# Zero-filled 128-row products for the 16-token block, and two shifted rope chains, in a four-layer hybrid kernel on one core

## The chip, the cores and the metric

The kernel runs on one core of a Trainium2 chip. The metric is the device time of one execution in microseconds. TensorE (PE) does the matrix products, VectorE (DVE), ScalarE (ACT) and GpSimd (POOL) the elementwise work, and SyncE (SP) issues the DMAs. In the profile the loading of a product's stationary operand (its weights) is a row of its own, PEld.

## The reference

1024 tokens are preceded by 16 learned meta tokens, so the sequence that counts has 1040 tokens, width 1024. Four layers follow each other; each adds its branch to the residual stream, and the 16 meta tokens are dropped at the end.

```python
h = concat(zeros(112), meta(16), x(1024))          # blocks of 128; the first holds 16 valid tokens
for i in range(4):
    u = rmsnorm(h, norm_gain[i])
    y = (attention_branch, mlstm_branch, hgrn2_branch)[i % 3](u, ...)
    h = h + where(valid, y, 0)
return h[:, 128:]

# attention (layers 0 and 3): 16 heads of 64, 4 k/v heads, window 128 inside and across blocks
q = rope(rmsnorm(q, q_gain), pos); k = rope(rmsnorm(k, k_gain), pos)
p = softmax over this block and the one before, with a sink per head
o = p @ v ;  y = (o * silu(z)) @ w_out
# mlstm (layer 1): 8 heads, keys 128, values 256, chunks of one block, state C (128 x 256) and n (128)
num = w_inter * (q @ C) + qk @ v ;  C = w_old * C + (w_s * k)^T @ v
# hgrn2 (layer 2): 8 heads, keys 128, values 128, state S (128 x 128)
o = (q * exp(A)) @ S + att @ v ;  S = exp(A_last) * S + k'^T @ v
```

## The kernel before

Everything is kept with channels on partitions and tokens on the free axis, in three chunks of tokens (400, 384 and 256 columns). The 1040 tokens are nine blocks: block 0 with the 16 meta tokens, blocks 1 to 8 with 128 tokens each (`blk(b)` gives a block's first column and its size, `cn` or `nq`). Chunk 0 holds blocks 0 to 3.

The large products (`proj`, line 231; `proj_v`, line 280; `proj_out`, line 325) run in three parts, high times high, low times high and high times low, with operands split by ACT (`s.copy` to a rounded type, line 195) and DVE (the remainder, line 196). Weights come by DMA into `wr` (line 207).

The mixers work block by block. For block 0 they use slices of 16 partitions or 16 columns:

- attention, `S_step`, `T_step`, `V_step`: `S_step` makes the scores and the normalised probabilities `Sm` (its last operation is POOL's line 737), `T_step` transposes them on PE (line 749) and splits them into `Ph` and `Pl` (ACT line 751, DVE line 752), `V_step` multiplies them with the values (line 768). In layer 0 this is done for block 0 of four pairs of tiles and two halves; layer 3 leaves block 0 out, because its queries are dropped.
- mlstm, `mixer` of `layer_b`: `s1` makes `W` and `kw`, `s2` multiplies `W` with the values (line 1010; for later blocks also the state, line 1012) and makes `hn`, `s3` makes the state's update from `kw` and the values (line 1024), `s4` transposes `hn` (line 1038).
- hgrn2, `mixer` of `layer_c`: `tail0` makes `att`, for block 0 in a 16x16 tile (line 1282), for the others by copies on POOL (line 1290, `att<-rd`); `kT` is the transposed key (line 1314); line 1322 makes the state's update and line 1343 the output.

The values of block 0 in layers 1 and 2 are written by `put_v` (lines 240 to 246).

PE's order is written out by hand: a layer gives lists of steps with a cost each, `chain` and `spread` put follow-up steps at a delay behind their tile, and `weave` merges lists by cost. The other engines' order follows from the order in which the steps are issued. The normalisation and rope of a k tile are three follow-up steps per chunk in `qk_proj`: `stat` (the sum of squares on PE, lines 614 and 617, and its reciprocal root on ACT, lines 341 and 342), `rope` (four DVE operations, lines 624 to 628) and `turn` (`k_split`: six ACT casts at lines 507, 508 and 510 and two DVE subtractions). Their delays behind the tile, in the units of the step costs, are `D_K0` for the first k tile of layer 0, `D_K1` for the second, and `D_K` for layer 3. For the second tile `stat` also issues the DMAs that swap halves (`turned`, line 568). The rows that a step's `stat` needs are ACT's two readings of the product, lines 574 and 575.

Of the kernel before, what the change touches and what calls it, by code (L numbers as in the profile page):

```python
# [9 lines left out]
F32 = mybir.dt.float32  # L10
# [36 lines left out]
FIRST = (1.1, 0.2, 0.85), (2.1, 1.35, 1.85)  # L47
D_K0, D_K1 = (2500.0, 5000.0, 7000.0), (4500.0, 7500.0, 9500.0)
D_Q0 = 3500.0, 7500.0, 4500.0, 6500.0
# [64 lines left out]
def hybrid_kernel(ctx: ExitStack, tc: tile.TileContext, ins, out, layers=(0, 1, 2, 3)):  # L114
# [125 lines left out]
    def put_v(V, acc, b, cn):  # L240

        if b == 0:
            s.copy(V[:cn, :256], acc[32 : 32 + cn, :256])
            v.tensor_tensor(V[:cn, :256], V[:cn, :256], acc[:cn, :256], op=ALU.add)
        else:
            s.copy(V[:cn, :256], acc[:cn, :256])
# [232 lines left out]
    def layer_a(i, j, first, last, fin, scale=None):  # L479
# [217 lines left out]
        def mixers():  # L697


            def S_step(w):  # L700
# [16 lines left out]
                S = psum("pm", 2).rearrange("p (u k) -> p u k", u=2)  # L717
                w["Sm"] = Sm = mix.tile([P, 2, 257], F32, tag="Sm", name=nm("Sm"), bufs=2)
                st, den = small(2), small(2)
                sinks = []  # L720
# [19 lines left out]
            def T_step(w):  # L740
                b, kbs, Sm = w["b"], w["kbs"], w["Sm"]
                nq = blk(b)[1]
                kn = NMETA if b == 0 else P
                pt = psum("pt", 1).rearrange("p (k u q) -> p k u q", k=2, u=2)
                w["Ph"] = Ph = R["mix"].tile([P, 2, 2, P], F32R, tag="Ph", name=nm("Ph"), bufs=2)
                w["Pl"] = Pl = R["mix"].tile([P, 2, 2, P], F32R, tag="Pl", name=nm("Pl"), bufs=2)
                for ki, (kb, ko, _) in enumerate(kbs):
                    for u in range(2):
                        pe.transpose(pt[:kn, ki, u, :nq], Sm[:nq, u, ko : ko + kn], ident[:nq, :nq])  # L749
                src, h, l = (z[:kn, : len(kbs), :, :nq] for z in (pt, Ph, Pl))  # L750
                s.copy(h, src)
                v.tensor_tensor(l, src, h.bitcast(F32), op=ALU.subtract)

            def V_step(w):
                b, kbs, hh, pair = w["b"], w["kbs"], w["hh"], w["pair"]
                q0, nq = blk(b)
                kn = NMETA if b == 0 else P
                grp = [z for z in GROUPS if b in z][0]
                g0 = blk(grp[0])[0]
                if b == grp[0]:  # L760
                    for t in w["ts"]:
                        if ("o", t) not in R:
                            R["o", t] = row()
                    R["po", hh] = psum("po", 1).rearrange("p (u q) -> p u q", u=2)
                po = R["po", hh]
                for ki, (kb, _, _) in enumerate(kbs):
                    for part in ("Ph", "Pl"):
                        pe.matmul(po[:, :, q0 - g0 : q0 - g0 + nq], V[pair // 2, kb][:kn, P * hh : P * hh + P],  # L768
                                  w[part][:kn, ki, :, :nq], start=(ki == 0 and part == "Ph"),
                                  stop=(ki == len(kbs) - 1 and part == "Pl"))  # L770
                if b == grp[-1]:
                    hs, os = slice(64 * hh, 64 * hh + 64), slice(64 - 64 * hh, 128 - 64 * hh)
                    gw = q0 + nq - g0
                    for u, t in enumerate(w["ts"]):
                        o = R["o", t][hs, g0 : g0 + gw]
                        s.copy(o, po[hs, u, :gw])
                        v.tensor_tensor(o, o, po[os, u, :gw], op=ALU.add)
# [80 lines left out]
    def layer_b(i, j, fin):  # L858
# [116 lines left out]
        def mixer(h):  # L975
# [8 lines left out]
            def s1(b):  # L984
# [10 lines left out]
                s.activation(E[:cn, :cn], E[:cn, :cn], AF.Exp)  # L995
                W["W", b] = w = mix.tile([P, P], F32, tag="W", name=nm("W"), bufs=2)
                v.tensor_tensor(w[:cn, :cn], E[:cn, :cn], pq[:cn, :cn], op=ALU.mult)
                if b:
                    W["qw", b] = qw = mix.tile([P, P], F32, tag="qw", name=nm("qw"), bufs=2)
                    v.tensor_tensor(qw, q[:, cs], R["wb"][:, cs], op=ALU.mult)  # L1000
                if b < NB - 1:
                    W["kw", b] = kw = mix.tile([P, P], F32, tag="kw", name=nm("kw"), bufs=2)
                    s.activation(kw[:cn], pq[:cn, 128:256], AF.Identity, scale=E[:cn, cn - 1 : cn])

            def s2(b):
                mix = R["mix"]
                c0, cn = blk(b)
                V = R["v", h, b]
                num = psum("po", 1)
                pe.matmul(num[:cn, :257], W["W", b][:cn, :cn], V[:cn, :257], start=True, stop=(b == 0))  # L1010
                if b:
                    pe.matmul(num[:cn, :257], W["qw", b], W["C"][:, :257], start=False, stop=True)  # L1012
                den = small(1)
                s.activation(den[:cn], num[:cn, 256:257], AF.Abs)
                v.tensor_tensor(den[:cn], den[:cn], R["em"][:cn, b, h : h + 1], op=ALU.max)
                v.reciprocal(den[:cn], den[:cn])
                W["hn", b] = hn = mix.tile([P, 256], F32, tag="hn", name=nm("hn"), bufs=2)
                s.activation(hn[:cn], num[:cn, :256], AF.Identity, scale=den[:cn])

            def s3(b):  # L1020
                mix = R["mix"]
                c0, cn = blk(b)
                pc = psa()
                pe.matmul(pc[:, :257], W["kw", b][:cn], R["v", h, b][:cn, :257], start=True, stop=True)  # L1024
                Cn = mix.tile([P, 258], F32, tag="C", name=nm("C"), bufs=2)
# [7 lines left out]
            def s4(b):  # L1033
# [3 lines left out]
                for c in range(2):  # L1037
                    pe.transpose(pt[:, c * P : c * P + cn], W["hn", b][:cn, c * P : c * P + P], ident[:cn, :cn])
                for c in range(2):
# [91 lines left out]
    def layer_c(i, j, fin):  # L1131
# [80 lines left out]
        def mixer(h):  # L1212
# [56 lines left out]
            def tail0(r):  # L1269
# [10 lines left out]
                if r == 0:  # L1280
                    att = R["mix"].tile([16, 16], F32, tag="att0", name=nm("att0"), bufs=1)
                    v.tensor_reduce(att, t6[:16, 0, f0:, :w].rearrange("p l t -> p t l"),
                                    axis=mybir.AxisListType.X, op=ALU.add)
# [22 lines left out]
            def tail1(r):  # L1306
                c0, cn = geom(r)
                bn = min(cn, P)
                pt = psum("pt", 1)
                W["kT", r] = kT = R["mix"].tile([P, 256], F32, tag="kT", name=nm("kT"), bufs=1)  # L1310
                for b in range(len(REGIONS[r])):
                    pe.transpose(pt[:bn, P * b : P * b + P], W["kA", r][:, P * b : P * b + bn], ident)
# [3 lines left out]
            def states(r):  # L1316
# [3 lines left out]
                for b in blocks:  # L1320
                    cn = blk(REGIONS[r][b])[1]
                    pe.matmul(pc[:, P * b : P * b + P], W["kT", r][:cn, P * b : P * b + P],
                              R["v", h // 2, REGIONS[r][b]][:cn, vs], start=True, stop=True)
                for b in blocks:
# [7 lines left out]
            def tail2(r, b):  # L1332
# [9 lines left out]
                att = W["att", r] if r == 0 else W["att", r][:, b, :]  # L1342
                pe.matmul(W["po"][:, oc], V[:cn, vs], att, start=True, stop=(r == 0))
                if r:
# [263 lines left out]
```

## Time and profile before

| | value |
|---|---|
| runs | 2605.04, 2612.66, 2618.38 us (median 2612.66) |
| profiled execution | 2608.14 us, of which the span is 2606.4 us |
| granted TensorE clock | 0.997 |
| PE, PEld busy | 98%, 95% of the span |
| DVE, ACT, POOL busy | 75%, 65%, 9% |

The span is the time from the first to the last instruction on the core; the profiled execution has 1.7 us around it. A row of a view by groups reads: line, engine, operation, output<-input by the program's names, the form (for PE the stationary operand's rows and columns, then the moving operand's rows and columns), the count, then busy time and mean nanoseconds of one, then the idle time of the engine just before these instructions and what ended it. "<-issue" is idle time in which the engine waited for nothing that the trace shows. A row of a timeline reads: start, length, engine, line, operation, and in brackets the idle time before it with its releaser. Within layer 1 (480 to 1500 us) PE is busy nearly without a break; most of its waits for other engines lie in layers 0, 2 and 3.

### The profile page before, as it was taken

To read this page: it belongs to the slowest core of one execution; us is meant where nothing else is said; L and a number is where in the kernel's file an instruction comes from. 1 tells how busy PE (TensorE), PEld (TensorE's weight loads), DVE (VectorE), ACT (ScalarE), POOL (GpSimd) and SP (SyncE) were. 2 spreads that over 40 slices of the span, in tenths; PEclk is the share of its full clock that TensorE was granted. 3 is DMA by queue.
4 is the path that set the end of the run, shared out by engine and by line. 5 is a ranking of instruction groups with operands and counts; after the bars stand their busy time and mean duration, and the time that the engine had idled before them with its cause. 6 is when DMAs were issued, how large, how long until landed. Compare 5 with 4: busy or idle time off the path is not lost.

```text
span 2606.4 us, 54443 instructions
## 1 busy us (share of the span) xinstructions
PE 2563.6 (98%) x20446; PEld 2486.9 (95%) x20446; DVE 1960.2 (75%) x5290; ACT 1696.1 (65%) x4434; POOL 238.9 (9%) x488
## 2 busy tenths in 40 slices
PE   8999999999999999999999999999999999999999
PEld 7998989999999999999999999999999999999999
DVE  7896898775656564747465688988888978887896
ACT  8866766566464645555545757877675857867772
POOL 0321231000000000000000000101000100321320
PEclk9999999999999999999999999999999999999999
DMA  5223212021111111111111111111111113212112
GB/s 157 62 67 93 57 44 69 30 67 58 42 53 46 49 45 54 41 58 41 50 44 54 50 35 34 34 34 34 38 38 34 34 51 88 64 44 84 56 42 77
DMA packets 86058, 140.21 MB, mean 54 GB/s; under 512 B 12425, under 2 KB 39186, under 8 KB 85794
## 3 DMA queue, kind: packets, MB, share of 16 engines
q1 hardware_dynamic: 85794, 136.73, 17.0%
q8 instruction: 161, 2.64, 0.4%
q14 instruction: 103, 0.84, 0.1%
HBM read 121.83 MB, written 4.27 MB: 48 GB/s over the span
## 4 chain that ended last, share of the span: by engine, by line
PE 79%; DVE 10%; ACT 7%; DMA 2%; issue 2%; POOL 0%; SPq 0%; DVEq 0%; ACTq 0%; POOLq 0%
PE pj L231 38%; PE pj L325 16%; PE pj L280 10%; PE po L768 2%; PE pt L749 2%; PE po L1010 1%; PE pa L1024 1%; PE po L1012 1%; DVE wl L196 1%; DVE Sm L731 1%; ACT Sm L734 1%; PE pm L723 1%; PE pm L724 1%; PE pj L276 1%; PE pm L1262 1%
## 5 line engine op out<-in xcount | busy, mean ns | idle before, releaser
L231 PE MATMUL pj<-uh,wh 128*128 128x256 f32 (+2 forms) x2688 | 915.0, 340 | 6.7 <-ACT uh L400 6.2
L231 PE MATMUL pj<-ul,wh 128*128 128x256 f32 (+2 forms) x2688 | 864.6, 322 | 0.3
L231 PE MATMUL pj<-uh,wl 128*128 128x256 f32 (+2 forms) x2688 | 864.8, 322 | 0.0
L231 PEld LDWEIGHTS pj<-uh,wh 128*128 128x128 f32 x2688 | 508.1, 189 | 23.1 <-issue 9.0
L231 PEld LDWEIGHTS pj<-ul,wh 128*128 128x128 f32 x2688 | 508.8, 189 | 6.0 <-DVE ul L196 0.8
L231 PEld LDWEIGHTS pj<-uh,wl 128*128 128x128 f32 x2688 | 507.9, 189 | 0.0
L196 DVE TENSOR_TENSOR wl<-wr,wh 128x512 fp32r<-128x512 f32 (+1 forms) x338 | 233.9, 701 | 52.4 <-ACT wh L195 48.9
L195 ACT CAST wh<-wr 128x512 fp32r<-128x512 f32 (+1 forms) x338 | 203.2, 613 | 101.4 <-PE pj L325 31.6
L325 PE MATMUL pj<-yh,wh 128*128 128x384 f32 (+2 forms) x768 | 253.7, 330 | 9.9 <-DVE x L328 7.8
L328 DVE TENSOR_TENSOR x<-x,pj 128x384 f32<-128x384 f32 (+2 forms) x480 | 234.8, 509 | 33.4 <-PE pj L325 32.1
L325 PE MATMUL pj<-yl,wh 128*128 128x384 f32 (+2 forms) x768 | 246.3, 321 | 0.1
L325 PE MATMUL pj<-yh,wl 128*128 128x384 f32 (+2 forms) x768 | 246.1, 320 | 0.0
L280 PE MATMUL pj<-wh,uh 128*128 128x256 f32 (+1 forms) x768 | 232.7, 303 | 0.0
L280 PE MATMUL pj<-wl,uh 128*128 128x256 f32 (+1 forms) x768 | 216.3, 282 | 0.0
L280 PE MATMUL pj<-wh,ul 128*128 128x256 f32 (+1 forms) x768 | 216.0, 281 | 0.0
L734 ACT ACTIVATE Sm<-Sm,s 128x257 f32<-128x257 f32 (+2 forms) x272 | 131.2, 484 | 84.6 <-DVE s L731 81.3
L737 POOL TENSOR_TENSOR Sm<-Sm,s 128x512 f32<-128x512 f32 (+2 forms) x136 | 139.4, 1025 | 419.0 <-DVE s L736 396.2
L457 ACT ACTIVATE t<-t 128x384 f32<-128x384 f32 (+2 forms) x240 | 117.8, 491 | 82.5 <-DVE t L456 80.4
L325 PEld LDWEIGHTS pj<-yh,wh 128*128 128x128 f32 x768 | 144.8, 189 | 14.1 <-DVE x L328 9.4
L195 ACT CAST yh<-r 128x384 fp32r<-128x384 f32 (+2 forms) x120 | 57.0, 478 | 149.9 <-PE pj L325 135.6
L280 PEld LDWEIGHTS pj<-wh,uh 128*128 128x128 f32 x768 | 144.7, 188 | 2.2
L280 PEld LDWEIGHTS pj<-wl,uh 128*128 128x128 f32 x768 | 144.9, 189 | 1.9
(287 smaller groups left out, 5404.5 us busy)
## 6 DMA issues: line engine op xcount, KB each, us to landing
wr<-in_b_win SPq DMA_DIRECT2D x124, 256.0 KB
wr<-in_a_win SPq DMA_DIRECT2D x80, 256.0 KB
wr<-in_c_win SPq DMA_DIRECT2D x64, 256.0 KB
wr<-in_a_wout SPq DMA_DIRECT2D x32, 256.0 KB
wr<-in_b_wout SPq DMA_DIRECT2D x32, 256.0 KB
t<-t SPq DMA_DIRECT2D x100, 48.0 KB
cs<-in_rope SPq DMA_DIRECT2D x11, 400.0 KB
cs<-in_rope SPq DMA_DIRECT2D x11, 384.0 KB
```

The lines of the kernel that those rows point to most:

```text
L195: s.copy(h, src)
L196: v.tensor_tensor(l, src, h.bitcast(F32), op=ALU.subtract)
L231: pe.matmul(acc[:, :cn], a[:, k, :], b[:, k, c0 : c0 + cn], start=(k == 0 and i == 0), stop=(k == KT - 1 and i == 2))
L276: pe.matmul(acc[:48, :nc], um[0][:, k, :], m[:, kk, :], start=(k == 0 and m is wh), stop=(k == KT - 1 and m is wl))
L280: pe.matmul(acc[:cn, :nc], a[:, k, c0 : c0 + cn], m[:, kk, :], start=(k == 0 and j == 0), stop=(k == KT - 1 and j == 2))
L325: pe.matmul(acc[:, :cn], a[:, k, mc], b, start=(k == 0 and i == 0), stop=(k == 1 and i == 2))
L328: v.tensor_tensor(x[:, m, c0 : c0 + cn], x[:, m, c0 : c0 + cn], acc[:, :cn], op=ALU.add)
L457: s.activation(a[:, :cn], a[:, :cn], AF.Exp)
L734: s.activation(Sm[:nq, u, : nk + 1], Sm[:nq, u, : nk + 1], AF.Exp, scale=-1.0, bias=st[:nq, u : u + 1], accum_out=den[:nq, u : u + 1])
L737: g.tensor_tensor(Sm[:nq, :, :nk], Sm[:nq, :, :nk], den[:nq].rearrange("p (u c) -> p u c", c=1).to_broadcast([nq, 2, nk]), op=ALU.mult)
L749: pe.transpose(pt[:kn, ki, u, :nq], Sm[:nq, u, ko : ko + kn], ident[:nq, :nq])
L768: pe.matmul(po[:, :, q0 - g0 : q0 - g0 + nq], V[pair // 2, kb][:kn, P * hh : P * hh + P], w[part][:kn, ki, :, :nq], start=(ki == 0 and par ...
```

## The change

The tiles that block 0's small products read are now filled with zeros by POOL (`g.memset`), and the products take all 128 partitions, and all 128 stationary columns where they took 16. The moving operand's number of columns stays, except at line 1038, a transposition, where it becomes 128. The evictions still read the 16 rows or columns that count. The delays `D_K0` and `D_K1` are changed. Lines move by 1 to 14 in the changed file.

```diff
-D_K0, D_K1 = (2500.0, 5000.0, 7000.0), (4500.0, 7500.0, 9500.0)
+D_K0, D_K1 = (4300.0, 6300.0, 8300.0), (4400.0, 5700.0, 8500.0)
...
         if b == 0:
+            g.memset(V, 0.0)
             s.copy(V[:cn, :256], acc[32 : 32 + cn, :256])
...
+                if b == 0:
+                    g.memset(Sm[:, :, :NMETA], 0.0)
...
+                if b == 0:
+                    for z in (Ph, Pl):
+                        g.memset(z[:, 0, :, :NMETA].bitcast(F32), 0.0)
...
-                        pe.transpose(pt[:kn, ki, u, :nq], Sm[:nq, u, ko : ko + kn], ident[:nq, :nq])
+                        pe.transpose(pt[:kn, ki, u, :], Sm[:, u, ko : ko + kn], ident)
...
-                        pe.matmul(po[:, :, q0 - g0 : q0 - g0 + nq], V[pair // 2, kb][:kn, P * hh : P * hh + P],
-                                  w[part][:kn, ki, :, :nq], start=(ki == 0 and part == "Ph"),
+                        pe.matmul(po[:, :, q0 - g0 : q0 - g0 + nq], V[pair // 2, kb][:, P * hh : P * hh + P],
+                                  w[part][:, ki, :, :nq], start=(ki == 0 and part == "Ph"),
...
+                if b == 0:
+                    g.memset(w, 0.0)
...
+                    if b == 0:
+                        g.memset(kw, 0.0)
...
-                pe.matmul(num[:cn, :257], W["W", b][:cn, :cn], V[:cn, :257], start=True, stop=(b == 0))
+                pe.matmul(num[:, :257], W["W", b], V[:, :257], start=True, stop=(b == 0))
...
+                if b == 0:
+                    g.memset(hn, 0.0)
...
-                pe.matmul(pc[:, :257], W["kw", b][:cn], R["v", h, b][:cn, :257], start=True, stop=True)
+                pe.matmul(pc[:, :257], W["kw", b], R["v", h, b][:, :257], start=True, stop=True)
...
-                    pe.transpose(pt[:, c * P : c * P + cn], W["hn", b][:cn, c * P : c * P + P], ident[:cn, :cn])
+                    pe.transpose(pt[:, c * P : c * P + P], W["hn", b][:, c * P : c * P + P], ident)
...
-                    att = R["mix"].tile([16, 16], F32, tag="att0", name=nm("att0"), bufs=1)
+                    att = R["mix"].tile([P, 16], F32, tag="att0", name=nm("att0"), bufs=1)
+                    g.memset(att, 0.0)
...
+                if r == 0:
+                    g.memset(kT[:, :P], 0.0)
...
-                    pe.matmul(pc[:, P * b : P * b + P], W["kT", r][:cn, P * b : P * b + P],
-                              R["v", h // 2, REGIONS[r][b]][:cn, vs], start=True, stop=True)
+                    pe.matmul(pc[:, P * b : P * b + P], W["kT", r][:, P * b : P * b + P],
+                              R["v", h // 2, REGIONS[r][b]][:, vs], start=True, stop=True)
...
-                pe.matmul(W["po"][:, oc], V[:cn, vs], att, start=True, stop=(r == 0))
+                pe.matmul(W["po"][:, oc], V[:, vs], att, start=True, stop=(r == 0))
```

POOL gets 76 more instructions, all of them memsets: 12 of `V` (128x258; 8 heads of layer 1, 4 pairs of layer 2), 8 of `Sm`, 16 of `Ph` and `Pl`, and 8 each of `W`, `kw`, `hn`, `att` and `kT`. PE has the same instructions in the same order, in the new forms, except for the `stat` steps of the two k tiles in layer 0.

The first place is PE in the first 30 us, chunk 0 of the first k tile. `pj_350` is its product for chunk 1 of the q tile before, `pj_433` (later `pj_424`) the next product, `L614` and `L617` the `stat` of the k tile's chunk 0 (`r_302`), `L597` sums for the q tiles. Before:

```order
L231 MATMUL pj_350<-uh,wl_91 128x384
L614 MATMUL pa_387<-r_302,masks_186 128x400
L617 MATMUL pa_387<-r_86,ones 128x400
L231 MATMUL pj_350<-uh,wh_90 128x384
L231 MATMUL pj_350<-ul,wh_90 128x384
L231 MATMUL pj_350<-uh,wl_91 128x384
L231 MATMUL pj_350<-uh,wh_90 128x384
L231 MATMUL pj_350<-ul,wh_90 128x384
L231 MATMUL pj_350<-uh,wl_91 128x384
L597 MATMUL pa_414<-masks_186,t_237 128x2 x4
L597 MATMUL pa_423<-masks_186,Pl_262 128x2 x4
```

After:

```order
L598 MATMUL pa_405<-masks_186,t_237 128x2 x4
L598 MATMUL pa_416<-masks_186,Pl_262 128x2 x4
L231 MATMUL pj_424<-uh,wh_104 128x384
L231 MATMUL pj_424<-ul,wh_104 128x384
L231 MATMUL pj_424<-uh,wl_105 128x384
L231 MATMUL pj_424<-uh,wh_104 128x384
L231 MATMUL pj_424<-ul,wh_104 128x384
L231 MATMUL pj_424<-uh,wl_105 128x384
L615 MATMUL pa_433<-r_302,masks_186 128x400
L618 MATMUL pa_433<-r_86,ones 128x400
L231 MATMUL pj_424<-uh,wh_104 128x384
```

The `stat` stood six products ahead of `L597`; it now stands behind both of them and six products of the next tile. Chunk 1 of this tile moves behind 18 products of 256 columns and one `L597`, chunk 2 behind 12 products. In the second k tile chunk 0's `stat` moves six 256-column products ahead, chunks 1 and 2 keep their place.

The second place is ACT where the first block-0 step of layer 0's mixer ends: `L734` is the exponential in `Sm`, `L751` the high part `Ph` for `V_step`, `r_301` the first k tile, whose chunk 2 is split by `L507`, `L508` and `L510`, `wh` a split of weights. Before:

```order
L734 ACTIVATE Sm_868,s_870<-Sm_868,s_869 16x17
L685 ACTIVATE v_843<-pt_828,scale 128x2x64
L734 ACTIVATE Sm_868,s_870<-Sm_868,s_869 16x17
L751 CAST Ph_891<-pt_890 16x2x16
L507 CAST r_477<-r_301 64x256
L508 CAST r_477<-r_301 64x256
L507 CAST r_479<-r_301 64x256
L751 CAST Ph_928<-pt_927 16x2x16
L510 CAST r_478<-r_478 64x256
```

After, each name one or more lines further down in the file:

```order
L195 CAST wh_932<-wr_934 128x512
L508 CAST r_488<-r_301 64x256
L195 CAST wh_932<-wr_938 128x512
L509 CAST r_488<-r_301 64x256
L511 CAST r_489<-r_489 64x256
L508 CAST r_490<-r_301 64x256
L509 CAST r_490<-r_301 64x256
L511 CAST r_491<-r_491 64x256
L757 CAST Ph_893<-pt_892 16x2x16
L757 CAST Ph_924<-pt_923 16x2x16
```

All six casts of the k tile's last chunk now stand ahead of the first `Ph`, where three of them stood behind the first and three behind the second, and two splits of weights (`wh_932`), which stood further ahead, stand there as well.

The third place is POOL in layer 2, from the end of the first head into the second: `att_20315` and `kT_20351` are block 0's tiles of the second head, `att_21419` that of the third, and `L1302` the copies `att<-rd` of the later blocks, four to a row. After:

```order
L1293 MEMSET att_20315 128x16
L1302 COPY att_18793<-rd_19540 32x2x32 x4
L1302 COPY att_18792<-rd_19737 32x2x32 x4
L1302 COPY att_18793<-rd_19941 32x2x32 x4
L1302 COPY att_18792<-rd_20149 32x2x32 x4
L1324 MEMSET kT_20351 128x128
L1293 MEMSET att_21419 128x16
L1302 COPY att_18793<-rd_20544 32x2x32 x4
```

The copies stood in the same order before, with nothing between them. The memset of a head's `kT` stands behind the last copies of the head before and ahead of the first copies of its own.

More of the change, by code (lines that the diff above doesn't have):

```diff
@@ L756, in V_step @@
                 q0, nq = blk(b)
-                kn = NMETA if b == 0 else P
                 grp = [z for z in GROUPS if b in z][0]
@@ L1280, in tail0 @@
                 if r == 0:
-                    att = R["mix"].tile([16, 16], F32, tag="att0", name=nm("att0"), bufs=1)
-                    v.tensor_reduce(att, t6[:16, 0, f0:, :w].rearrange("p l t -> p t l"),
+                    att = R["mix"].tile([P, 16], F32, tag="att0", name=nm("att0"), bufs=1)
+                    g.memset(att, 0.0)
+                    v.tensor_reduce(att[:16], t6[:16, 0, f0:, :w].rearrange("p l t -> p t l"),
                                     axis=mybir.AxisListType.X, op=ALU.add)
```

## The prediction

> **What bounds the kernel now.** I read the page's busy times and chain first, then the busy time by stretch, then PE's waits.
>
> ```profile
> span 2606.4 us, 54443 instructions
> PE 2563.6 (98%) x20446; PEld 2486.9 (95%) x20446; DVE 1960.2 (75%) x5290; ACT 1696.1 (65%) x4434; POOL 238.9 (9%) x488
> PE 79%; DVE 10%; ACT 7%; DMA 2%; issue 2%; POOL 0%; SPq 0%; DVEq 0%; ACTq 0%; POOLq 0%
> 480.00:1500.00 1020.00, 1019.89 (x6760) 993.78 (x6758) 622.02 (x1579) 581.09 (x1380) 7.04 (x66) 1.00 0.16 50
> ```
>
> TensorE carries the chain. In layer 1, the last row (length, then busy time of PE, PEld, DVE, ACT and POOL), PE lacks 0.11 us of 1020, and the other engines have slack: whatever shortens PE's own stream there is gained in full. But "busy" is not "at its peak": the stream can lose time between two products without a row that says so. Where PE waits, the view of waits names the releasers (total, times, longest):
>
> ```profile
> PE pt L749 <- POOL Sm L737: 6.9, 6, 1.9
> PE pa L614 <- ACT r L575: 4.2, 3, 1.7
> PE pa L614 <- ACT t L575: 3.0, 1, 3.0
> ```
>
> The two rows of L614 are what the shifted delays address: 7.2 us.
>
> **The padded products: what one group of 16 rows costs.** The timeline of PE in layer 1, around block 0 of one head (L1010, then L1024), and around a later block of another (two pairs, L1010 and L1012):
>
> ```profile
> 546.41 0.34 PE L231 MATMUL pj<-uh,wl 128*128 128x400 f32 x1
> 546.68 0.60 PE L1010 MATMUL po<-v,W 16*16 16x257 f32 x2
> 547.21 0.45 PE L231 MATMUL pj<-uh,wh 128*128 128x400 f32 x1
> 547.50 0.34 PE L231 MATMUL pj<-ul,wh 128*128 128x400 f32 x1
> ...
> 549.13 0.34 PE L231 MATMUL pj<-ul,wh 128*128 128x400 f32 x1
> 549.32 0.34 PE L231 MATMUL pj<-uh,wl 128*128 128x400 f32 x1
> 549.59 0.70 PE L1024 MATMUL pa<-v,kw 16*128 16x257 f32 x2
> 550.22 0.44 PE L231 MATMUL pj<-uh,wh 128*128 128x384 f32 x1
> 550.50 0.34 PE L231 MATMUL pj<-ul,wh 128*128 128x384 f32 x1
> ```
>
> ```profile
> 675.92 0.34 PE L231 MATMUL pj<-uh,wl 128*128 128x384 f32 x1
> 676.09 0.60 PE L1010 MATMUL po<-v,W 128*128 128x257 f32 x2
> 676.52 0.60 PE L1012 MATMUL po<-C,qw 128*128 128x257 f32 x2
> 676.77 0.53 PE L231 MATMUL pj<-uh,wh 128*128 128x384 f32 x1
> 677.14 0.34 PE L231 MATMUL pj<-ul,wh 128*128 128x384 f32 x1
> ```
>
> Large products start 0.18 us apart (549.13 to 549.32, rounded). From the last one before a group to the second one behind it there would be two such steps, 0.36 us, without the group. The 16-row L1010 makes it 1.09 us (546.41 to 547.50), so it costs 0.73; L1024 makes it 1.18, so it costs 0.82. The two 128-row pairs make it 1.22, so they cost 0.86, 0.43 a pair, with eight times the rows and, in L1010, eight times the weight columns. The excess is 0.30 and 0.39 us. It lies at the edges: the first weight load of a 16-row group does not start under the product before, and the first large one behind it starts late too. The groups of PEld show the first of these edges as idle time (behind the second bar, with what ended it):
>
> ```profile
> L1010 PEld LDWEIGHTS po<-v,W 16*16 16x16 f32 x16 | 0.8, 89 | 2.1 <-issue 2.1
> L1024 PEld LDWEIGHTS pa<-v,kw 16*128 16x128 f32 x16 | 2.3, 182 | 2.0 <-issue 2.0
> L1322 PEld LDWEIGHTS pa<-v,kT 16*128 16x128 f32 x16 | 2.3, 183 | 2.0 <-ACT t L1177 0.5 <-issue 0.5 <-ACT X L1238 0.5
> L1343 PEld LDWEIGHTS po<-att,v 16*128 16x128 f32 x16 | 2.3, 182 | 1.9 <-issue 1.0 <-DVE X L1236 0.3 <-DVE X L1239 0.3
> L1038 PEld LDWEIGHTS pt<-ident,hn 16*128 16x128 f32 x16 | 1.6, 135 | 1.2 <-ACT t L457 0.3
> L768 PEld LDWEIGHTS po<-Ph,v 16*128 16x128 f32 x8 | 1.4, 181 | 1.6 <-DVE s L731 0.5 <-issue 0.3 <-DVE Pl L752 0.2
> L749 PEld LDWEIGHTS pt<-ident,Sm 16*16 16x16 f32 x16 | 0.8, 84 | 3.1 <-POOL Sm L737 1.9 <-issue 1.0
> ...
> L1024 PEld LDWEIGHTS pa<-v,kw 128*128 128x128 f32 x112 | 17.9, 189 | 0.0
> L1312 PEld LDWEIGHTS pt<-ident,X 128*16 128x16 f32 x8 | 0.7, 88 | 0.0
> ```
>
> All seven groups of 16 rows have it; with 128 rows there is none, also with only 16 columns (L1312). So it goes with the rows, and that is what the change removes.
>
> The sum. L1010 and L1024 occur once for each of 8 heads: 8 x 0.30 + 8 x 0.39 = 5.5 us, 1.35 times their idle 4.1. I take the other five groups by that ratio, L749 with its "issue" part alone (its wait for POOL stays): 2.0 + 1.9 + 1.2 + 1.6 + 1.0 = 7.7, times 1.35 is 10.4. If every named releaser there was a real wait, which padding would not remove, 2.6 goes off and 6.9 is left. I take the middle, 8.7, an estimate. Together **14.2 us, between 12.4 and 15.9**. The wider loads (89 to some 189 ns in L1010) are in these numbers, since the 128-row pair has them.
>
> [...]
>
> **The memsets.** 76 more instructions on POOL. The nearest rows are a memset of the same size as `V`, and what stands in POOL's way in layer 2, with the product that a late `kT` would hold up:
>
> ```profile
> L679 POOL MEMSET v<- 128x258 f32 x4 | 1.3, 314 | 0.3 <-POOLq L1599 0.3
> 1649.55 1.44 POOL L1290 COPY att<-rd 32x64 f32<-32x64 f32 x4 [11.82 <-DVE rd L1288]
> 1670.54 3.88 POOL L1290 COPY att<-rd 32x64 f32<-32x64 f32 x4 [19.55 <-DVE rd L1288]
> 1662.56 0.48 PE L1322 MATMUL pa<-v,kT 16*128 16x128 f32 x2
> ```
>
> At 0.31 us or less each they are under 24 us on an engine that is busy for 9%. In layers 1 and 2 the tiles come free a head ahead, and the order puts each memset ahead of POOL's long waits: cost 0. In layer 0 those of `Ph` and `Pl` are issued in the step that fills them, behind what POOL has queued; 8 steps, and only the first few with PE waiting nearby: I take 0.3 us, from 0 up to 1.6 (16 of them at 0.1 us, an estimate: a third of L679's 258 columns' time or less for 32 columns).
>
> **First k tile later.** PE waits 4.2 us for ACT's L575. In the new order chunk 0's L614 stands behind twelve more large products (12 x 0.18 = 2.1 us) and eight sums, chunk 1's behind 18 of 256 columns (18 x 0.12 = 2.1, the 0.18 scaled by columns) and chunk 2's behind twelve; each is more than the longest of the three waits, 1.7, so they go. What is late next is ACT, which does the same work in a stretch where it has little to spare:
>
> ```profile
> 65.00:80.00 15.00, 13.94 (x104) 12.75 (x104) 12.52 (x49) 12.71 (x48) 2.85 (x7) 1.00 0.31 98
> ...
> 65.08 0.62 ACT L195 CAST wh<-wr 128x512 fp32r<-128x512 f32 x1
> 70.81 0.17 ACT L751 CAST Ph<-pt 16x32 fp32r<-16x32 f32 x1
> 70.89 0.40 ACT L507 CAST r<-r 64x256 fp32r<-64x256 f32 x1
> ```
>
> Before the second `Ph` of the first mixer step ACT now has three more casts of 0.41 us and two weight splits of 0.62 us: 2.5 us. If `V_step` waits for all of it, 4.2 - 2.5 = **1.7 us** are left. The ends are 0 (PE arrives sooner and waits for ACT by as much) and 4.2; the row of 12.71 busy in 15 us makes me take the low part.
>
> **Second k tile.** Before, the 3.0 us wait ended a row of late steps: half-swapping DMA behind a weight transfer on SP, rope, and then ACT's L574 and L575 of chunk 2.
>
> ```profile
> 233.35 0.53 SPq L207 DMA_DIRECT2D wr<-in_a_win x1
> ...
> 236.89 0.58 DVE L624 TENSOR_TENSOR t<-t,cs 128x400 f32<-128x400 f32 x1 [6.05 <-DMA t<-t]
> ```
>
> Chunk 0's `stat` comes six 256-column products sooner, 6 x 0.12 = 0.7 us, and the last of its swaps passes one weight transfer (0.53 us): **1.2 us** of 3.0. The ends are 0 and 3.0. The weight transfer that is passed is late by as much; its split had waited for DMA anyway, and that is in the low end.
>
> **The sum**: 14.2 + 1.7 + 1.2 - 0.3 = 16.8 us off the profiled 2608.14, 2591.3. The median of the runs is 2612.66, so this is 2591.3 x 2612.66 / 2608.14 = **2596 us**. The bounds added (12.4 + 0 + 0 - 1.6 to 15.9 + 4.2 + 3.0) are 10.8 and 23.1.
>
> **Rivals.**
>
> *Rows are not what costs.* If the edges come from the change of the stationary operand's place or form as such, and a padded group has them too, only the moved chains are left: 1.7 + 1.2 - 0.3 = 2.6 us, 2610. For it: the loads themselves take the same with 16 rows as with 128 (182 and 189 ns). Against it: the 0.43 against 0.82 us, with the same 257 columns, between the same large products. Chance 0.11. [...]
>
> *A wait takes the place of the one removed.* ACT's queue, or the memsets of `Ph` and `Pl`, give back all of both k gains in layer 0, and the named releasers in layer 2 were real: 12.4 - 1.6 = 10.8 us, 2602. For it: ACT's 12.71 us in 15. Against it: waits of that size would stand at two places only. Chance 0.16.
>
> *Slower: the memset of `kT` waits behind the copies.* If POOL reaches a head's `kT` memset only behind the first copies of that head, L1322's 16-row pair, which ran at 1662.56, waits for their end at 1670.54 + 3.88 = 1674.42: 11.9 us in each of 7 heads, 83 us, less the 16.8 is 66 us more, 2679. It decides when the memset's row stands behind those copies in POOL's order; the order shows it ahead, behind the copies of the head before, which began at 1649.55 and took 1.44. Chance 0.04.
>
> **How the numbers follow.** The forecast has 0.66, the rivals 0.11, 0.16 and 0.04, and 0.03 is left for more than the sum's upper end. 0.5% is 13.1 us, about what a measurement of this kernel can tell from no change; faster by more is below 2599.6. Of the forecast's span (gains of 11 to 23 us) about nine tenths lie below: 0.59 + 0.03 = 0.62 faster. Within 0.5% are the rest, 0.07 + 0.11 + 0.16 = 0.34. Slower is 0.04. The range 2586 to 2607 holds the forecast and the rival of the returned waits, with the runs' own scatter; it leaves out the first rival, the slower one and the 0.03, 0.18 in all.
>
> **What would show it.** Right: the groups of L1010, L1024, L1322, L1343, L1038, L768 and L749 in block 0 have 128 rows, and their PEld rows no idle time but waits for data; layer 1 alone is about 7 us shorter (5.5, and 1.2 x 1.35 for L1038); the rows of L614 waiting for L575 are gone or below 3 us in all. Wrong: PEld idle on "issue" before the padded groups; new waits of L768 for `Ph` or `Pl` of more than 3 us; a wait of L1322 or L1010 for POOL; or layer 1 with the same length.

## The result, and the profile after

The changed kernel took 2598.27 us (median of 6 runs, 2596.0 to 2599.1) beside 2612.1 us of the kernel before (6 runs, 2605.04 to 2618.38): 0.9948 of its time, 95% interval 0.993 to 0.9966, so some 14 us less (9 to 18). Run again beside the last experiments it came to 0.9955 (0.9941 to 0.9969). The profiled execution took 2596.91 us, 11.2 us less than the profiled one before.

The page's first lines of the changed kernel, span and busy times:

```profile
span 2595.1 us, 54389 instructions
PE 2547.2 (98%) x20446; PEld 2486.5 (96%) x20446; DVE 1960.2 (76%) x5290; ACT 1689.9 (65%) x4434; POOL 245.6 (9%) x564
```

PE has the same number of instructions and 16.4 us less busy time; POOL has its 76 memsets more, for 6.7 us.

The groups of PEld in the changed kernel show what became of the idle time ahead of the 16-row products, which now count with the 128-row ones (L1019 was L1010, L1035 was L1024, L1336 was L1322, L1357 was L1343, L755 was L749):

```profile
L1357 PEld LDWEIGHTS po<-att,v 128*128 128x128 f32 x144 | 24.6, 193 | 2.2 <-POOL att L1302 2.2
L1019 PEld LDWEIGHTS po<-v,W 128*128 128x128 f32 x144 | 23.9, 189 | 0.3 <-DVE W L1004 0.3
L1035 PEld LDWEIGHTS pa<-v,kw 128*128 128x128 f32 x128 | 20.9, 189 | 0.0
L1336 PEld LDWEIGHTS pa<-v,kT 128*128 128x128 f32 x128 | 19.0, 190 | 7.8 <-ACT kT L1328 7.8
...
L755 PEld LDWEIGHTS pt<-ident,Sm 128*16 128x16 f32 x16 | 1.3, 88 | 3.6 <-POOL Sm L740 3.1
```

The idle time on "issue" is gone in all of them. Of the two groups not shown, L773 (was L768) has 1.7 us left, 1.5 of it waiting for `Ph`, and L1049 (was L1038) 1.1, which its 128-row loads had before too. What is left waits for data, and in one row there is more of it: `kT` is 7.8 us, where the 128-row loads of the kernel before had 3.9.

```profile
L1322 PEld LDWEIGHTS pa<-v,kT 128*128 128x128 f32 x112 | 16.1, 190 | 4.1 <-ACT kT L1314 3.9
```

The timeline of PE at the same two groups of the first head in layer 1:

```profile
544.35 0.34 PE L231 MATMUL pj<-uh,wl 128*128 128x400 f32 x1
544.52 0.59 PE L1019 MATMUL po<-v,W 128*128 128x257 f32 x2
544.77 0.53 PE L231 MATMUL pj<-uh,wh 128*128 128x400 f32 x1
545.14 0.34 PE L231 MATMUL pj<-ul,wh 128*128 128x400 f32 x1
...
546.97 0.34 PE L231 MATMUL pj<-uh,wl 128*128 128x400 f32 x1
547.16 0.59 PE L1035 MATMUL pa<-v,kw 128*128 128x257 f32 x2
547.40 0.52 PE L231 MATMUL pj<-uh,wh 128*128 128x384 f32 x1
547.76 0.34 PE L231 MATMUL pj<-ul,wh 128*128 128x384 f32 x1
```

From the last large product before a group to the second behind it are 0.79 us now, where 1.09 and 1.18 were; less the two steps of 0.18 a group costs 0.43, the price of the later blocks' pairs. Layer 1 shows the sum. The row of L231 ahead of the first group stands at 544.35, where it stood at 546.41: PE is 2.06 us ahead there. At the layer's end the sums of the last tile, before and then after:

```profile
1491.12 0.44 PE L1083 MATMUL pa<-yl,onesr 128*128 128x384 f32 x1
```

```profile
1482.49 0.44 PE L1094 MATMUL pa<-yl,onesr 128*128 128x384 f32 x1
```

PE is 8.63 us ahead, so layer 1 gave 6.6. PE's waits in the changed kernel, total, times and longest:

```profile
PE pt L755 <- POOL Sm L740: 10.7, 10, 2.2
...
PE pa L1336 <- ACT kT L1328: 5.3, 6, 1.9
...
PE pa L615 <- ACT t L576: 1.8, 1, 1.8
PE po L773 <- ACT Ph L757: 1.3, 1, 1.3
```

The first k tile's 4.2 us are gone, the second's 3.0 are 1.8. New are 1.3 us for `Ph`, 3.8 us more for `Sm` and 3.3 more for `kT`.

One thing more differs. The busy time by stretch (length, then PE, PEld, DVE, ACT and POOL with their instructions, then the granted clock), of the kernel before, and of the changed one, around the second k tile's wait:

```profile
242.38:245.80 3.42, 1.84 (x7) 1.18 (x8) 2.49 (x5) 2.43 (x7) 0.00 (x0) 1.00 0.47 136
245.80:249.21 3.41, 3.41 (x14) 3.21 (x13) 1.67 (x4) 2.93 (x8) 0.00 (x0) 0.50 0.16 54
```

```profile
245.80:249.21 3.41, 3.41 (x24) 3.33 (x23) 1.69 (x6) 3.30 (x9) 0.00 (x0) 1.00 0.29 86
```

Before, PE got half its clock for 3.41 us behind the wait, and issued 14 products in a stretch where it issues 24 at the full clock.

### The profile page after: what moved, and what is told of

The parts are those of the page before. It is cut to its first block, busy times and chain, and to the rows that moved or that the text cites. A ratio compares the mean times of both kernels' runs of the same rounds, so it can differ in the third digit from the quotient of the medians.

```text
span 2595.1 us, 54389 instructions
## 1 busy us (share of the span) xinstructions
PE 2547.2 (98%) x20446; PEld 2486.5 (96%) x20446; DVE 1960.2 (76%) x5290; ACT 1689.9 (65%) x4434; POOL 245.6 (9%) x564
## 4 chain that ended last, share of the span: by engine, by line
PE 65%; DVE 13%; ACT 9%; issue 2%; DMA 2%; POOL 0%; SPq 0%; DVEq 0%; ACTq 0%; POOLq 0%
PE pj L231 29%; PE pj L326 15%; PE pj L281 10%; DVE wl L196 1%; ACT Sm L737 1%; PE po L1019 1%; PE po L1021 1%; PE pa L1035 1%; DVE Sm L734 1%; PE po L773 1%; ACT wh L195 1%; PE pt L755 1%; ACT X L1249 1%; PE pj L277 1%; DVE t L457 1%
## 5 line engine op out<-in xcount | busy, mean ns | idle before, releaser
L231 PE MATMUL pj<-uh,wh 128*128 128x256 f32 (+2 forms) x2688 | 914.8, 340 | 6.9 <-ACT uh L401 6.4
L231 PE MATMUL pj<-ul,wh 128*128 128x256 f32 (+2 forms) x2688 | 864.2, 322 | 0.3
L231 PE MATMUL pj<-uh,wl 128*128 128x256 f32 (+2 forms) x2688 | 864.3, 322 | 0.0
L231 PEld LDWEIGHTS pj<-uh,wh 128*128 128x128 f32 x2688 | 507.4, 189 | 16.3 <-ACT uh L401 6.4
L231 PEld LDWEIGHTS pj<-ul,wh 128*128 128x128 f32 x2688 | 507.9, 189 | 6.4 <-DVE ul L196 0.9
L231 PEld LDWEIGHTS pj<-uh,wl 128*128 128x128 f32 x2688 | 507.2, 189 | 0.0
L326 PEld LDWEIGHTS pj<-yh,wh 128*128 128x128 f32 x768 | 144.5, 188 | 14.0 <-DVE x L329 10.4
L457 DVE SCALAR_TENSOR_TENSOR t<-pj,t 128x400 f32<-128x400 f32 (+2 forms) x168 | 86.5, 515 | 81.6 <-ACT t L456 80.3
```

Source lines behind the costliest of these rows:

```text
L231: pe.matmul(acc[:, :cn], a[:, k, :], b[:, k, c0 : c0 + cn], start=(k == 0 and i == 0), stop=(k == KT - 1 and i == 2))
L326: pe.matmul(acc[:, :cn], a[:, k, mc], b, start=(k == 0 and i == 0), stop=(k == 1 and i == 2))
L457: v.scalar_tensor_tensor(a[:, :cn], z, 0.0, a[:, :cn], op0=ALU.min, op1=ALU.subtract)
```

## The experiments

Theory 1 is the prediction's own sum: padding 14.2 us, the first k tile 1.7, the second 1.2. Theory 2 came from laying the two traces side by side: padding counts in full in layer 1 alone, in layers 0 and 2 waits for other engines take most of it back, and the delays work through stretches of half clock. "Lead" is the time by which PE starts a product earlier than in the profile of the kernel before. Ratios are to the kernel before on the same chip, with 95% intervals; in microseconds a thousandth is 2.6.

### Padding without the delays, delays without the padding

`e1_pads`: the change without

```diff
-D_K0, D_K1 = (2500.0, 5000.0, 7000.0), (4500.0, 7500.0, 9500.0)
+D_K0, D_K1 = (4300.0, 6300.0, 8300.0), (4400.0, 5700.0, 8500.0)
```

> All zero-filled products, the delays D_K0 and D_K1 as before. By the prediction the padding carries the gain: 14.2 us off, some 2598. By the reading of the two traces it brings 6.5 us in layer 1, about 2 in layer 2, and nothing in layer 0, some 2603; what is left of the measured 13.8 us is then the delays and stretches of lower granted clock.

Measured: 0.9969 (0.9956 to 0.9983), 8.1 us less. `e2_delays` is those two lines alone:

> Only D_K0 and D_K1 changed, no zero fill. By the prediction 1.7 + 1.2 = 2.9 us off, 2609. By the reading of the two traces the first k tile gives nothing (the mixer's first steps give it back) and the second 1.2 us of wait and up to 1.7 us of a stretch at half clock behind that wait, also 2609 to 2611. They differ in the trace: PE's lead at 76 us should be 1.7 us by the first and 0 or less by the second.

Measured: 0.9975 (0.9966 to 0.9983), 6.5 us less, twice what either theory allowed. The two parts add up to the change as first measured (14.6 us against 14; measured again it was 11.7). PE's lead at 76 us is minus 0.8 us in its trace, which looks like theory 2. But this execution was behind from its start: L432, ahead of every step that moved, starts at 23.17 us, where it started at 21.51. From minus 1.7 to minus 0.8, some 0.9 us of lead is kept, between the 1.7 of theory 1 and the 0 of theory 2.

### The two delays apart

`e3_k0` takes only `D_K0` from the change.

> Only D_K0 changed. By the prediction 1.7 us off; by the traces a lead of 4.2 us on PE at 62 us that is gone by 76 us, where the high part Ph waits behind six casts of the k tile and a split of weights on ScalarE: 0, perhaps 1 us slower.

Measured: 0.9988 (0.9979 to 0.9997), 3.1 us less. Most of the lead is given back. The rows are a large product that comes after the k tile's third `stat` in both orders, and the first wide transposes of the mixer, in the kernel before and in this one.

```profile
65.36 0.42 PE L231 MATMUL pj<-uh,wh 128*128 128x384 f32 x1
...
75.72 0.27 PE L749 MATMUL pt<-ident,Sm 128*128 128x128 f32 x1
```

```profile
61.34 0.42 PE L231 MATMUL pj<-uh,wh 128*128 128x384 f32 x1
...
75.38 0.33 PE L749 MATMUL pt<-ident,Sm 128*128 128x128 f32 x1 [0.97 <-POOL Sm L737]
```

4.0 us of lead are 0.3 at 76 us. This execution too was behind from its start, by 0.6 us (L432 at 22.06), so some 0.9 us is kept. Its profile has half clock from 68.6 to 72.0 us, but that is not what takes the lead: the changed kernel's profile has none there and arrives at 76 us with minus 0.3, from minus 0.7 at its start. The runs are faster by 0.8 to 5.5 us, which theory 2 did not say. `e4_k1` takes only `D_K1`.

> Only D_K1 changed. By the prediction 1.2 us off and PE's wait of 3.0 us for L575 down to 1.8. By the reading of the traces the same wait, and no stretch of half clock behind it: 1.2 + 1.6 = 2.8 us off.

Measured: 0.9992 (0.9983 to 1.0001), 2.1 us less, with no change just inside the interval. In the trace the wait is 2.24 instead of 3.00 us, PE's lead goes from minus 0.4 us at 235 us to plus 1.9 at 252, and there is no half clock there: 0.8 us of wait and 1.5 of clock. This pair of traces does not show that `D_K1` did it. The kernel before happened to have the longest wait: the other seven profiles with the old `D_K1` have 2.1 to 2.4 us, and three of them (`e5_padB`, `e7_padA`, `e8_memsets`) no half clock there either and the same gain of 2.4 us over these steps. The row in `e7_padA`:

```profile
PE pa L614 <- ACT t L575: 2.1, 1, 2.1
```

The six profiles with the new `D_K1` have 1.4 to 2.2 us, some 0.5 less in the mean, and two of them (`e2_delays`, `e11_poolk`) have half clock behind the wait, as five of the eight old ones do. The runs agree with fewer such stretches: their mean granted clock is 0.9970, that of the kernel before beside them 0.9960 (a difference of 0 to 0.002).

### One layer at a time

`e5_padB` has the padded products of layer 1 alone, with old delays.

> Zero fill and 128-row products in layer 1 alone (V, W, kw, hn; L1010, L1024, L1038), delays as before. By the prediction 5.5 + 1.6 = 7.1 us off, by the two traces 6.5; in both the gain grows in eight equal steps of 0.3 to 0.4 us at L1010 and at L1024 and is there at the end. If the rows were not what costs: 0.

Measured: 0.9978 (0.9966 to 0.9991), 5.7 us less. In its trace PE is 3.1 us behind the kernel before at 480 us and 3.7 ahead at 1500: 6.8 us in layer 1, in equal steps at L1010 and L1024. `e6_padC` pads layer 2 alone.

> The same in layer 2 alone (V, att, kT; L1322, L1343), delays as before. By the prediction (2.0 + 1.9) x 1.35 = 5.3 us off, 3.2 if every named releaser was a real wait. By the reading of the traces 2 to 3 us, since PE arrives sooner at products that wait for kT of the later blocks, which does not come sooner.

Measured: 0.9987 (0.9977 to 0.9998), 3.4 us less. Its trace gains 3.0 us between 1500 and 2100 us. The wait for `kT`, before and here:

```profile
PE pa L1322 <- ACT kT L1314: 2.0, 4, 0.9
```

```profile
PE pa L1327 <- ACT kT L1319: 4.8, 8, 1.2
```

That is 2.8 us more of it. Not all of the 3.0 us is padding: this profile lacks a stretch of half clock that the kernel before has at 1631 us, and `e2_delays` and `e3_k0`, which lack it too and have no padding here, gain 1.0 us over the same span. So some 1.9 us is kept, and PE's own stream was shortened by about 4.7. `e7_padA` pads layer 0 alone.

> The same in layer 0 alone (Sm, Ph, Pl; L749, L768), delays as before. By the prediction (1.6 + 1.0) x 1.35 - 0.3 = 3.2 us off, 1.9 with real waits. By the reading of the traces nothing or 1 us slower: what PE gains up to 150 us goes again at 155 to 165 us, where ScalarE and VectorE do block 0's parts of a later pair behind other work.

Measured: 0.9996 (0.9982 to 1.001), no difference. In its trace PE gains 1.1 us between 76 and 150 us and loses 1.5 between 150 and 235, all of it at 160 us. `e8_memsets` puts in the memsets and keeps the old products:

```diff
+                    g.memset(w, 0.0)
...
-                att = W["att", r] if r == 0 else W["att", r][:, b, :]
+                att = W["att", r][:cn] if r == 0 else W["att", r][:, b, :]
```

> All 76 memsets, the products in their old forms of 16 rows, delays as before. By the prediction 0.3 us slower, at most 1.6. If the memsets shift the order of ScalarE and VectorE in layer 0, as the traces suggest, 1 to 2 us slower, all of it at 155 to 165 us; in layers 1 and 2 nothing by either.

Measured: 1.0008 (0.9997 to 1.0018), 2.1 us slower with no change just inside the interval. Where the time should have gone by the expectation is wrong: its trace loses nothing at 155 to 165 us, nor in layers 1 and 2. It is the wide products that move the other engines' work: against the kernel before, the first 600 rows of VectorE's order show 6 rows of difference with the memsets alone and 52 with layer 0 padded, most of them around `Pl` of block 0 in a later pair, at 137 to 156 us, just ahead of the loss. No run kept the old order with the wide products, so the moved order is the likely cause, not a shown one.

### What stands behind the first k tile's waits

The traces of `e5_padB`, `e6_padC` and `e8_memsets`, all with the old `D_K0`, have a stretch that the profile before does not have. By stretch, first `e5_padB`, then `e6_padC`:

```profile
26.40:29.80 3.40, 2.07 (x6) 0.93 (x7) 0.99 (x2) 3.17 (x9) 0.00 (x0) 1.00 0.33 86
29.80:40.00 10.20, 10.20 (x39) 10.20 (x38) 5.39 (x14) 5.82 (x16) 0.00 (x0) 0.50 0.21 55
```

```profile
46.30:49.70 3.40, 1.66 (x9) 0.91 (x8) 2.91 (x7) 3.33 (x9) 0.00 (x0) 1.00 0.13 34
49.70:59.90 10.20, 10.20 (x44) 9.13 (x45) 7.25 (x15) 5.11 (x15) 0.61 (x1) 0.50 0.22 68
```

Half clock for 10.24 us, right behind the wait for L575 of chunk 0 or chunk 1. Between 20 and 76 us these three lost 4.7 to 6.5 us against the profile before (e5 and e8 have one more stretch of 3.41 us at 54 us). Of the seven profiles with the old `D_K0` and no filler (before, e1, e4 to e8) three have it, of the six with the new one (the change twice, e2, e3, e11, e12) none. If that share holds, 3 of 7 times some 5.9 us is 2.5 us on average, most of e3's 3.1; but 3 of 7 against 0 of 6 can be chance. And four of the six new ones have a stretch of 3.41 us of their own at 68 to 75 us; three of these cost nothing (`e2_delays`, `e3_k0`, `e10_after` keep as much lead past 78 us as the changed kernel without one), that of `e12_best` cost 1.2 us.

The granted clock of the single runs does not bear that share out. `e3_k0` has the mean clock of the kernel before beside it, 0.9960 in 11 and in 35 runs (a difference of up to 0.0008 either way), and takes less time at the same clock: at 0.997 2603.9 us (3 runs) beside 2606.7 (18). So for e3's 3.1 us some 0.9 us of lead is shown, and the rest stays open. `e9_fill` asks whether it is the idle PE that does it, and not the place of the steps:

```diff
                     st = psa()
+                    if scaled and not fetched:
+                        for _ in range((2, 2, 1)[n]):
+                            pe.matmul(st[:, :256], R["masks"][:, 0:P], R["masks"][:, 0:256], start=True, stop=True)
```

> The kernel before, and ahead of L614 in the three chunks of the first k tile 2, 2 and 1 additional products of 256 columns, whose output nobody reads: they stand where PE waited 1.6, 1.7 and 0.8 us. If the delay D_K0 gains because these waits bring stretches of half clock behind them (10 us at 30 or 50 us in some profiles), PE is no longer idle there, no such stretch comes before 65 us, and the time falls by 2 to 4 us, with no move of the k tile's steps. If the waits themselves are what costs, nothing changes, or 1 us slower.

Measured: 0.999 (0.9979 to 1.0), 2.7 us less by the medians, with five products more and the k tile's steps where they were; its highest run is 2608.68, the highest of before 2615.79. Its one profile has no half clock before 244 us, and the longest waits left for L575 are 0.8 and 0.9 us. That fits the idle PE as the cause of the half clock. The interval of the time reaches no change, but the granted clock of the runs is clear: 0.9973 in the mean of these 12, 0.9958 in the 21 of the kernel before beside them (a difference of 0.0005 to 0.0025), and at the same clock the two take about the same time (at 0.997 2607.3 us in 6 runs and 2606.7 in 4). So the fillers gain by the clock, which the runs do not show for `D_K0`.

### Keeping what was given back

`e10_after` is the changed kernel again.

> The changed kernel again, beside the others: 0.993 to 0.997 of before.

Measured: 2597.49 us, 0.9955 (0.9941 to 0.9969). `e11_poolk` moves four casts of the last chunk of the first k tile to GpSimd:

```diff
+                        cp = g.tensor_copy if first and j == 0 and n == 2 else s.copy
                         s.copy(kh[hs, cs], k[hs])
-                        s.copy(kh[os, cs], k[hs])
+                        cp(kh[os, cs], k[hs])
                         v.tensor_tensor(kl[hs, cs], k[hs], kh[hs, cs].bitcast(F32), op=ALU.subtract)
-                        s.copy(kl[os, cs], kl[hs, cs].bitcast(F32))
+                        cp(kl[os, cs], kl[hs, cs].bitcast(F32))
```

> The changed kernel, with four of the six casts of the first k tile's chunk 2 on GpSimd, which is idle there, instead of ScalarE. If the lead of 4.2 us at 62 us is given back because Ph waits behind these casts, L768's wait of 1.3 us for Ph goes, and PE keeps 1 to 2 us at 76 us: 1 to 2 us below the changed kernel. If VectorE's rope or the weights are what is late, nothing changes.

Measured: 2596.9 us, 0.9953 (0.9939 to 0.9967), not to be told from the changed kernel. In the trace the reason holds. First the changed kernel, ACT's end of the six casts and PE's wait for them, then PE in this one:

```profile
72.87 0.40 ACT L511 CAST r<-r 64x256 fp32r<-64x256 f32 x1
73.18 0.24 ACT L757 CAST Ph<-pt 16x32 fp32r<-16x32 f32 x2
...
73.40 0.28 PE L773 MATMUL po<-Ph,v 128*128 128x32 f32 x1 [1.34 <-ACT Ph L757]
```

```profile
72.08 0.28 PE L774 MATMUL po<-Ph,v 128*128 128x32 f32 x1
72.98 0.28 PE L774 MATMUL po<-Pl,v 128*128 128x32 f32 x1 [0.62 <-DVE Pl L759]
```

The wait for `Ph` is gone and 0.6 us for `Pl` takes its place: 0.6 us kept, not 1 to 2. `e12_best` adds fillers at three waits of 2.1 to 2.2 us:

```diff
+                if (w["pair"], b, w["hh"]) in (((0, 1, 0),) if last else ((0, 0, 0), (3, 7, 1))):
+                    z = psa()
+                    for _ in range(2):
+                        pe.matmul(z[:, :256], R["masks"][:, 0:P], R["masks"][:, 0:256], start=True, stop=True)
```

> As the run before, and 2 products of 256 columns that nobody reads ahead of three transposes of T_step that wait 2.1 to 2.2 us for GpSimd's Sm (first step of layer 0, the step of pair 3, block 7, second half, and the first step of layer 3). If stretches of half clock follow only where PE is idle for some 1.9 us of a 3.41 us window, none follows at these three places, and 0 to 3 us more are gained: 2592 to 2596. If not, nothing, or 1 us slower.

Measured: 2595.63 us, 0.9946 (0.9931 to 0.9961), the lowest of all, but with an interval that holds the changed kernel's. The three places behave as expected. The first of them by stretch, in `e10_after` and then here:

```profile
64.20:67.60 3.40, 1.23 (x10) 0.88 (x9) 3.03 (x17) 3.40 (x17) 0.82 (x3) 0.99 0.02 7
67.60:71.00 3.40, 3.40 (x19) 3.25 (x18) 2.65 (x7) 1.66 (x5) 2.05 (x3) 0.50 0.74 209
```

```profile
64.60:68.00 3.40, 2.09 (x14) 1.61 (x13) 3.11 (x15) 3.09 (x16) 1.12 (x2) 1.00 0.01 2
68.00:71.40 3.40, 3.01 (x25) 2.69 (x23) 2.64 (x6) 1.68 (x5) 2.43 (x4) 1.00 0.81 245
```

1.23 us of PE's time in 3.40 was followed by half clock (0.50), 2.09 was not (1.00). But stretches of half clock came at other places in that profile, at 74.8, 344, 2174 and 2467 us, so this one profile gains nothing in sum. Over the runs the mean granted clock is 0.9982, beside 0.9968 in `e10_after`.

## Why the prediction was right, and where it was not

The time, 2598.27 against 2596 forecast, and the sign are right, and the main step, that the rows are what costs, is shown: the edges on "issue" are gone, a group costs 0.43 us, and the first rival (rows are not what costs, 2610) is out. L755, now 128 rows by 16 columns, has no idle time on "issue" left to speak of (0.5 of its 3.6 us is not POOL's). The prediction's "with 128 rows there is none" holds for the rows shown there and not for every form: in the profile before, L1252's 512 loads of 128x32 have 2.5 us on "issue" and L1262's 64 of 128x16 have 1.5. The slower rival's place is as the order showed it: no product of block 0 waits for a memset in the view of waits. But two terms of the sum were off by several microseconds, padding too high and delays too low, and that the total came within 3 us is in part luck.

- **Layer 1** (5.5 and L1038's share): forecast about 7, measured 6.6 in the trace of the change and 6.8 alone, give or take 0.6, by which profiles without padding differ from the kernel before over this span. Right.
- **Layer 2**: the step "I take the other five groups by that ratio" priced PE's own stream about rightly, (2.0 + 1.9) x 1.35 = 5.3 against 4.7 in `e6_padC`, but counted it as gained. More than half, 2.8 us, came back as waits for `kT`, which does not come sooner. The prediction had asked whether the named releasers were real waits; the waits that count stood at the later blocks' products.
- **Layer 0**: the same step gave about 3 us for L768 and L749 with their memsets. The trace of `e7_padA` gains 1.1 and loses 1.5 us at 160 us, and the runs show no difference. The likely reason is that the wide products also moved ACT's and DVE's order, which the prediction read only at the first pair.
- **Memsets**: forecast 0.3 us, measured 2.1 with 0 just inside the interval. The trace shows no place for more than 1 us; where the rest would be is open.
- **First k tile**: the step "4.2 - 2.5 = 1.7 us are left" was too high for the lead, of which some 0.9 us is kept in `e3_k0`. The runs gain 3.1 us (0.8 to 5.5), at the same mean clock; where the rest comes from is open.
- **Second k tile**: 1.2 us forecast out of a wait of 3.0, which was the longest of eight. Against the other seven the wait is some 0.5 us shorter, and the half clock behind it, 1.5 us, comes less often, but is not gone.

So 14.2 of padding are 8.1 (4.4 to 11.5), and 2.9 of delays are 6.5 (4.4 to 8.9). Of these 6.5, 0.9 us of lead and 0.5 of wait are shown; `e2_delays` runs at a clock higher by 0.0011, which by the price at the end of this document is some 2.5 us, an estimate; some 2.6 us stay open. The second rival, a wait in place of the one removed, is in part what happened in layers 0 and 2; what it did not see is that a wait of PE cost more than its length where half clock followed it: behind the second k tile's 3.0 us before, the stretch of 3.41 us at 245 us cost 1.5. Of the 11.2 us between the two profiled executions, some 4 to 5 are stretches of half clock that one has and the other has not: at 245, 2184 and 2478 us before, at 2093 after. The last of these four stands behind a wait that the change made longer (`kT`, 1.9 us there); the one at 245 comes and goes without the change as well, and the other two are not of its making.

## What to carry to other kernels

A pair of products on 16 rows cost 0.30 and 0.39 us more here than a pair on 128 (L1010, L1024): look for weight loads that sit idle on "issue" ahead of narrow products, and price zero-filling from the pitch of the large products around them. Count such a gain only where PE is the last to arrive; where a product waited for another engine it came back as a wait (2.8 us for `kT` in `e6_padC`), and where the order of the other engines moved, most likely too (1.5 us at 160 us in `e7_padA`). And waits of PE of about 2 us cost more than their length here where half clock followed, 1.0 to 1.6 us for each stretch of 3.41 us, so filling them with products that nobody reads may gain though PE arrives no sooner (`e9_fill`: mean granted clock 0.9973 beside 0.9958, and a time of 0.999 with no change just inside the interval). Read such a gain from the granted clock of many runs: the stretches come and go from profile to profile, the one at 245 us in five of the eight with the old `D_K1`.

## What the runs showed of the hardware

The granted clock in these traces is at half (0.50) for 3.41 us or a multiple of it, and the stretches of one trace lie on a grid of 3.41 us: in the profile before they start at 245.80, 1631.61, 2184.57 and 2478.11 us, 406, 162 and 86 steps apart, in the one after at 1622.79 and 2093.83, 138 steps apart. The grid's phase to the kernel's start differs between the two: 245.80 is 0.04 us past a whole number of steps, 1622.79 is 1.46. I divided all 14 traces into that grid and summed PE's idle time in each window, from the first record of the clock on, 9 to 13 us into each trace (in the profile before at 10.28 us; products of 400 columns start 0.33 us apart ahead of it and 0.18 behind it). All 34 windows with 1.91 us or more were followed by half clock. Of 171 with 1.0 to 1.9 us, 14 were, nine of them at the k tiles' steps, among products of two columns or one row (L597, L617). The same wait can lie in one window in one run and in two in the next: the wait of 2.16 us for L328 near the end lay in one window in the profile before (2474.70 to 2478.11 us) and was followed by half clock; in the one after it is as long, lies in two windows with 0.79 and 1.37 us of idle time, and was not.

Less idle time stood ahead of half clock as well: in three profiles (`before`, `e6_padC`, `e12_best`) 6.83 us of half clock at 2174 to 2186 us followed a window with 0.72 to 0.75 us. There products of 256 columns start 0.29 us apart in the mean (2182.07 to 2184.71 us in the profile before), where 0.12 is their pitch elsewhere, so PE may be idle for longer than its busy time says; this was not tested.

A stretch of 3.41 us cost about 1.0 to 1.6 us where PE was the bound, the long one of 10.24 us in `e6_padC` 4.7. Against the profile after, the one before loses 1.5 us over each of its stretches at 245 and 2478 us, and 3.1 over the 6.83 us at 2184. Whole runs show the same price: of 89 runs of the kernel before, beside the experiments, the 36 with a mean granted clock of 0.997 took 2606.7 us in the mean, the 23 with 0.995 2611.3. That is 4.6 us for 0.002, or for some 10.4 us at half clock: 1.5 us for each 3.41, an estimate from these means.
